# A two-layer encoder trunk: who updates x and applies norm weights at the layer boundaries

## Chip, cores and metric

One core of a Trainium2 chip. The metric is the device time of one execution, in microseconds; the comparison is between two programs that compute the same output. Engines: TensorE (PE, with its weight loads PEld), VectorE (DVE), ScalarE (ACT), GpSimd (POOL) and the queues that issue transfers (SyncE's is SP).

## The reference, cut to what matters

256 tokens with 2048 features pass two layers. Each layer has two sublayers: a mixer (GLA and neighbourhood attention in layer 0, a state-space mixer and sliding-window attention in layer 1) with one input and one output projection, and a dense SwiGLU feed-forward part (FFN). Each sublayer is normed on both sides:

```
for layer in range(2):
    h = rms_norm(x, g[0]);  mix = concat(mixers(h @ w_in)) @ w_out
    x = x + rms_norm(mix, g[1])
    h = rms_norm(x, g[2]);  f = (silu(h @ w_gate) * (h @ w_up)) @ w_down
    x = x + rms_norm(f, g[3])

def rms_norm(x, g):
    return x * rsqrt(mean(x * x, axis=-1) + 1e-6) * g
```

So there are four places where a projection's output is normed and added to x, and after the first three of them the new x is at once the input of the next norm. These three are the layer boundaries below.

## The kernel before

**Number format and tiles.** All products are float32 in accuracy: every operand is split into `hi` (rounded to the reduced float32 format, fp32r) and `lo` (the rest), and three matmuls stand for one: hi·hi, hi·lo, lo·hi. The tokens are two halves of 128 (t=0 and t=1); an x tile of one half has four pieces of 512 features (j = 0 to 3).

**Weights.** They are streamed from memory in chunks of 512 x 512, in order of use, in halves of 128x1024. `prep()` takes the next half in: `halves` casts it on ACT (`whi`, L199) and subtracts on VectorE (`wlo`, L201). `whi` and `wlo` have seven buffers each, so a cast may wait until TensorE has used an older half. `unit_a` runs the matmuls of one 512-column output: for each chunk the ones of t=0 (`part(0, ...)`, L227 to L229, 12 per chunk) are issued at once; the ones of t=1 are kept in a list (`pending`), up to four half chunks (6 matmuls each) behind.

**The end of a sublayer** (`post`). The output comes in four quarters (n = 0 to 3) per half. When a quarter of the last pass is done, `evac` adds it to `f` on VectorE (L444), sums its squares on ACT (L361) and multiplies it in place by the norm's weights `gb` (L492, on POOL for most quarters). With the fourth, `rstd` gets the scale `rs[t]`: a reduction and a mean on VectorE (L352, L356) and a power on POOL (L357). Then each piece of x is updated: x = x + rs·f (L465 ff.).

**The next norm** (`begin_norm`, `piece`). A generator of three steps per piece: four transposes on TensorE into one of four PSUM tiles (`tp`, L343); a product with the weights of the next norm on VectorE (`gx`, L385) and a cast to `hi` on ACT (`xt`, L387); a subtraction to `lo` on VectorE (`xt`, L390), with the sum of squares on ACT. The row scale of the next norm is applied behind its projection. At the start of the program the same generator runs for the input x, without an update of x (`START`).

**Order.** At a boundary the order is written by hand in `PROG`: X/x is the update of a piece, T/t its transposes, G/g the product and cast, L/l the subtraction, in capitals for t=0; `p` is one `prep()`, `q` the next half chunk that is pending. The first string runs at the end of the sublayer, the third after two chunks of the next stage. Which engine updates x is written in `XMODE` (d: one VectorE instruction; p: product and sum on POOL; a: product on ACT, sum on POOL; the third string is for t=1 of the very last sublayer). `pin` holds marked TensorE and VectorE instructions in program order during a boundary; the rest, all of ACT and POOL among it, is put in order by a planner of the framework, which follows priorities and its own estimates of time.

**Transfers.** Each updated piece of x is written to memory from the POOL queue (`xm`, `xf`) and read back by the end of the next sublayer; in the last sublayer it is the output, written from SP's queue.

Of the kernel before, what the change touches and what calls it, by code (L numbers as in the profile page):

```python
# [18 lines left out]
F32 = mybir.dt.float32  # L19
# [3 lines left out]
ALU = mybir.AluOpType  # L23
# [3 lines left out]
P = 128  # L27
# [23 lines left out]
LAG = 2  # L51
PSTT, PADD, PY, AY = (1, 2), True, True, 1
SY = 2
XMODE, MULP = ("ddpd", "daaa", "dadd"), True
PROG = ("X0 X1 p p X2 q X3 T0 q G0 T1 q G1 q T2 L0 p L1 x1 T3 x2 x3 G2 p p L2 G3 x0 p L3",
        "", "t0 t1 g0 l0 g1 t2 l1 g2 t3 l2 g3 l3")
START = ("T0 T1 G0 G1 L0 p L1", "t0", "g0 t1 l0 g1 l1", "p", "T2 T3 G2 G3 L2 t2 L3 t3", "g2 l2 g3 l3")
CONST_PARTS = {
# [36 lines left out]
class Trunk:  # L95
# [267 lines left out]
    def begin_norm(self, li, gi):  # L363

        nc = self.nc
        xt = ([None] * 4, [None] * 4, [None] * 4)
        rs = [None, None]
        ssp = [None, None]
        gain = self.gT[:, li * 2 + gi // 2]

        def piece(t, j, src):
            if xt[0][j] is None:
                xt[2][j] = self.s8.tile([P, 2, 4, T], F32R, tag="s8", name=self.nm("xt"))
                xt[0][j], xt[1][j] = xt[2][j][:, 0], xt[2][j][:, 1]
            if j == 0:
                ssp[t] = self.small([P, 4], "nss", "nss")
                rs[t] = self.keep.tile([P, 1], F32, tag="nrs", bufs=4, name=self.nm("nrs"))
            sl = slice(t * P, (t + 1) * P)
            hi, lo = xt[0][j][:, :, sl], xt[1][j][:, :, sl]
            with self.tc.high_priority(offset=NORM):  # L380
                ps = self.transpose4(src)
            yield
            with self.tc.high_priority(offset=NORM):
                gx = self.tmp([P, 4, P], nm="gx")
                self.pin(nc.vector.tensor_tensor(out=gx, in0=ps, in1=gain[:, 4 * j:4 * j + 4].unsqueeze(2)  # L385
                                                 .broadcast_to([P, 4, P]), op=ALU.mult))
                self.pin(nc.scalar.copy(hi, gx))  # L387
            yield
            with self.tc.high_priority(offset=NORM):
                self.pin(nc.vector.tensor_sub(lo, gx, hi.bitcast(F32)))  # L390
            self.sumsq(src, ssp[t][:, j:j + 1])
            if j == 3:
                self.rstd(ssp[t], 4, D, rs[t])
        return xt, rs, piece
# [13 lines left out]
    def post(self, li, gi, nseg, after, f=None, before=None):  # L408


        nc = self.nc
        given = f is not None
        f = f or [[None, None], [None, None]]
        gb = [None] * 4
        ssp = [self.small([P, 4], "pss", "pss") for _ in range(2)]
        rs = [self.small([P, 1], "prs", "prs") for _ in range(2)]
        state = {"si": 0}

        def reload():
            self.x = [[None, None], [None, None]]  # L420
            for t in range(2):
                for j in range(2):
                    self.load_x(t, j, nc.gpsimd)

        def seg(mk, xk):
            si = state["si"]
            state["si"] += 1
            last = si == nseg - 1
            if last:
                if before is None:  # L430
                    reload()
                for n in range(4):
                    gb[n] = self.mtmp([P, 512], nm="gb")
                    self.tc.keep_in_program_order(nc.gpsimd.dma_start(  # L434
                        out=gb[n], in_=self.dr["norm_gains"][li, gi, n * 512:(n + 1) * 512].partition_broadcast(P)))

            def add(t, ps, n, pin=False):
                if f[t][n // 2] is None:
                    f[t][n // 2] = self.slot([P, 1024], nm="f")
                d = f[t][n // 2][:, (n % 2) * 512:(n % 2) * 512 + 512]  # L440
                if si == 0 and not given:
                    nc.scalar.copy(d, ps)
                else:
                    i = nc.vector.tensor_add(d, d, ps)  # L444
                    if pin:
                        self.pin(i)
                return d

            live = {}

            def run(prog):

                for c in prog.split():
                    if c == "p":
                        self.prep()
                        continue
                    if c == "q":
                        self.pending.popleft()()
                        continue
                    t, j = int(c[0].islower()), int(c[1])  # L460
                    if c[0] not in "Xx":
                        if live[t, j] is not None:
                            next(live[t, j], None)
                        continue
                    s2 = slice((j % 2) * 512, (j % 2) * 512 + 512)  # L465
                    xs, d = self.x[t][j // 2][:, s2], f[t][j // 2][:, s2]
                    with self.tc.high_priority(offset=NORM):
                        mode = XMODE[2 if li == 1 and gi == 3 and t else t][j]
                        if mode != "d":
                            if mode == "a":  # L470
                                nc.scalar.mul(d, d, rs[t])
                            else:
                                nc.gpsimd.tensor_scalar(out=d, in0=d, scalar1=rs[t], scalar2=None, op0=ALU.mult)
                            nc.gpsimd.tensor_add(out=xs, in0=xs, in1=d)
                        else:
                            self.pin(nc.vector.scalar_tensor_tensor(out=xs, in0=d, scalar=rs[t], in1=xs,
                                                                    op0=ALU.mult, op1=ALU.add))
                        live[t, j] = after(t, j, xs)

            for n in range(4):  # L480
                def evac(t, ps, n=n):
                    if not last:
                        return add(t, ps, n)
                    if n == 3 and t == 0:
                        self.prep()
                        self.pinning = ("PE", "DVE")
                    with self.tc.high_priority(offset=NORM):
                        d = add(t, ps, n, n == 3)
                        self.sumsq(d, ssp[t][:, n:n + 1])
                        if n == 3:  # L490
                            self.rstd(ssp[t], 4, D, rs[t])
                        i = (nc.gpsimd if n < 3 or (t and MULP and not (li == 1 and gi == 3)) else nc.vector).tensor_mul(out=d, in0=d, in1=gb[n])  # L492
                        if n == 3:
                            self.pin(i)
                    if n == 3 and t == 0:
                        self.pinning = ("PE",)
                        self.pending.popleft()()
                        self.pending.popleft()()
                        self.pinning = ("PE", "DVE")
                if before is not None:  # L500
                    before(n)
                    if n == 2:
                        reload()
                if last and n == 2:
                    self.pinned = {}
                    self.pinning = ("PE",)
                self.unit_a(mk(n), xk, evac, len(mk(n)) - 1 if n == 1 else None)
            if last:
                run(PROG[0])
                assert not self.pending  # L510

                def end():
                    run(PROG[2])
                    self.pinning = ()
                self.pending.extend((lambda: run(PROG[1]), lambda: None, end, lambda: None))
        return seg
# [977 lines left out]
```

## Time and profile before

| | |
|---|---|
| median of 3 runs | 2202.31 us (2201.97 to 2202.34) |
| the profiled execution | 2202.5 us, span 2200.6 us |
| busy: PE / PEld / DVE / ACT / POOL | 2163.8 / 1804.1 / 1741.3 / 1212.2 / 212.9 us |
| mean granted clock of TensorE | 0.996 |
| the boundaries | about 417 to 450, 1132 to 1166 and 1464 to 1497 us |
| the last x update | 2191.6 to 2194.7 us |

The span is the time between the first and the last instruction of the profiled execution. An engine's busy time counts its instructions alone; a busy TensorE may still be at the lower of its two clocks (1.0 is 2.4 GHz, 0.5 is 1.2 GHz). In a row of the timeline the numbers are start and duration in us; a bracket gives the idle time of the engine ahead of it and what ended it. Instructions of one engine can overlap by some 0.1 us, and rows with xN are N instructions of one kind that follow one another.

### The profile page before, as it was taken

How to read it: one execution, taken by the hardware profiler on the slowest of the kernel's cores; microseconds unless marked ns; L12 is line 12 of the kernel's file. 1: busy time of each engine (PE TensorE's matmuls, PEld its weight loads, DVE VectorE, ACT ScalarE, POOL GpSimd, SP SyncE). 2: the span in 40 equal slices, each digit the busy share in tenths (PEclk: the TensorE clock that was granted, in tenths of full speed). 3: DMA queues.
4: the chain of work that ended last, by engine and by line, in shares of the span. 5: the costliest groups of instructions: out<-in, count | busy, mean ns of one | idle time of the engine just before them, and what ended most of it. 6: DMA issues, size and time to landing. Idle time of an engine off the chain costs nothing.

```text
span 2200.6 us, 28141 instructions
## 1 busy us (share of the span) xinstructions
PE 2163.8 (98%) x10416; PEld 1804.1 (82%) x10416; DVE 1741.3 (79%) x2119; ACT 1212.2 (55%) x1533; POOL 212.9 (10%) x246
## 2 busy tenths in 40 slices
PE   8999999999999999999999999999999999999997
PEld 7888888778888888888878988778888888888886
DVE  7888655766878888888878987776687889888885
ACT  6545445555565555556456455655556555555653
POOL 0001110310000000000031262221000000000003
PEclk9999999999999999999999999999999999999999
DMA  8444565574565655467466444557466565646744
GB/s 294 144 134 162 189 200 187 184 267 149 204 238 182 207 175 202 172 219 243 150 215 230 152 153 143 179 186 269 148 204 239 176 209 166 215 172 217 242 153 143
DMA packets 117321, 424.48 MB, mean 193 GB/s; under 512 B 13392, under 2 KB 13520, under 8 KB 117184
## 3 DMA queue, kind: packets, MB, share of 16 engines
q1 hardware_dynamic: 110592, 400.61, 53.8%
q0 software_dynamic: 6448, 21.99, 3.0%
q8 instruction: 81, 1.33, 0.2%
q14 instruction: 56, 0.46, 0.1%
q10 hardware_dynamic: 144, 0.10, 0.0%
HBM read 414.25 MB, written 8.39 MB: 192 GB/s over the span
## 4 chain that ended last, share of the span: by engine, by line
PE 92%; DVE 4%; issue 2%; ACT 1%; POOL 1%; DMA 0%; DVEq 0%; SPq 0%; POOLq 0%; ACTq 0%
PE acc L229 21%; PE acc L227 21%; PE acc L228 21%; PE sq L703 5%; PE sq L702 5%; PE sq L704 5%; PE acc L260 4%; PE acc L263 2%; DVE wlo L201 2%; PE tp L343 1%; DVE xt L390 1%; PE gs L903 1%; PE accb L300 1%; PE accb L301 1%; PE accb L302 1%
## 5 line engine op out<-in xcount | busy, mean ns | idle before, releaser
L201 DVE TENSOR_TENSOR wlo<-raw,whi 128x1024 fp32r<-128x1024 f32 x608 | 755.7, 1249 | 291.1 <-ACT whi L199 283.1
L199 ACT CAST whi<-raw 128x1024 fp32r<-128x1024 f32 x608 | 638.4, 1053 | 608.2 <-PE acc L229 399.0
L229 PE MATMUL acc<-whi,xt 128*128 128x512 f32 x1760 | 689.2, 392 | 7.9 <-DVE xt L390 7.9
L228 PE MATMUL acc<-wlo,xt 128*128 128x512 f32 x1760 | 686.9, 391 | 0.0
L227 PE MATMUL acc<-whi,xt 128*128 128x512 f32 x1760 | 678.8, 392 | 4.2 <-ACT xt L387 3.2
L229 PEld LDWEIGHTS acc<-whi,xt 128*128 128x128 f32 x1760 | 331.4, 188 | 79.8 <-DVE xt L390 11.1
L227 PEld LDWEIGHTS acc<-whi,xt 128*128 128x128 f32 x1760 | 331.6, 188 | 73.8 <-ACT xt L387 5.3
L228 PEld LDWEIGHTS acc<-wlo,xt 128*128 128x128 f32 x1760 | 331.4, 188 | 69.3 <-DVE wlo L201 0.8
L199 ACT CAST whi<-sw 128x1024 fp32r<-128x1024 f32 x252 | 265.7, 1054 | 207.4 <-PE acc L229 136.5
L201 DVE TENSOR_TENSOR wlo<-sw,whi 128x1024 fp32r<-128x1024 f32 x252 | 305.5, 1221 | 55.4 <-ACT whi L199 52.3
L703 PE MATMUL sq<-wlo,so 128*128 128x512 f32 x504 | 196.1, 389 | 0.0
L704 PE MATMUL sq<-whi,so 128*128 128x512 f32 x504 | 196.1, 389 | 0.0
L702 PE MATMUL sq<-whi,so 128*128 128x512 f32 x504 | 195.8, 390 | 0.0
L651 DVE TENSOR_TENSOR sw<-sw,sw 128x1024 f32<-128x1024 f32 x144 | 174.6, 1220 | 14.7 <-DMA sw<-sstream 14.0
L260 PE MATMUL acc<-xt,whi 128*128 128x512 f32 x384 | 138.0, 404 | 0.0
L434 POOL DMA_DIRECT2D gb<-norm_gains x16 | 8.7, 546 | 1194.0 <-DVE so L618 1180.9
L704 PEld LDWEIGHTS sq<-whi,so 128*128 128x128 f32 x504 | 94.6, 188 | 19.6
L702 PEld LDWEIGHTS sq<-whi,so 128*128 128x128 f32 x504 | 94.6, 188 | 19.4
L703 PEld LDWEIGHTS sq<-wlo,so 128*128 128x128 f32 x504 | 94.6, 188 | 19.4
L263 PE MATMUL acc<-xt,wlo 128*128 128x256 f32 x384 | 105.8, 286 | 0.0
L227 PE MATMUL acc<-whi,mixh 128*128 128x512 f32 x256 | 98.5, 396 | 0.6 <-ACT sz L788 0.6
L229 PE MATMUL acc<-whi,mixl 128*128 128x512 f32 x256 | 97.9, 391 | 0.0
(276 smaller groups left out, 2361.6 us busy)
## 6 DMA issues: line engine op xcount, KB each, us to landing
raw<-wstream SPq DMA_DIRECT2D x612, 512.0 KB, 4.8
sw<-sstream SPq DMA_DIRECT2D x144, 512.0 KB, 6.4
gb<-norm_gains POOLq DMA_DIRECT2D x16, 256.0 KB, 4.4
xm<-x POOLq DMA_DIRECT2D x16, 256.0 KB, 3.3
x<-xm POOLq DMA_DIRECT2D x8, 512.0 KB, 5.9
x<-x SPq DMA_DIRECT2D x4, 512.0 KB, 8.4
x<-x POOLq DMA_DIRECT2D x4, 512.0 KB, 7.4
xf<-x POOLq DMA_DIRECT2D x8, 256.0 KB, 3.4
```

The lines of the kernel that those rows point to most:

```text
L199: self.pin(nc.scalar.copy(hi, src))
L201: self.pin(nc.vector.tensor_sub(lo, src, hi.bitcast(F32)))
L227: self.pin(nc.tensor.matmul(ps[t], xh, wh[:, k % 2], start=s, stop=False))
L228: self.pin(nc.tensor.matmul(ps[t], xh, wl[:, k % 2], start=False, stop=False))
L229: self.pin(nc.tensor.matmul(ps[t], xl, wh[:, k % 2], start=False, stop=e))
L260: wide = lambda s, e: nc.tensor.matmul(ps, wh[:, kt % 8], self.joined(kt, xt), start=s, stop=e)
L263: nc.tensor.matmul(ps[:, 0], wl[:, kt % 8], xt[0][kt // 4][:, kt % 4, :], start=False, stop=False)
L300: nc.tensor.matmul(ps, wh[:, kt % 8], xh, start=kt == 0, stop=False)
L651: nc.vector.tensor_add(a, a, b)
L702: nc.tensor.matmul(ps, xh, wh[:, k], start=s, stop=False)
L703: nc.tensor.matmul(ps, xh, wl[:, k], start=False, stop=False)
L704: nc.tensor.matmul(ps, xl, wh[:, k], start=False, stop=e)
```

## The change

All updates of x are one VectorE instruction each (`XMODE` is gone). The products with `gb` of the quarters n=2 and 3 are on VectorE for both halves, n=0 and 1 stay on POOL (`MULP` is gone). In `piece` the weights of the next norm are no longer applied by a separate product: ACT makes `hi` from the transposed PSUM tile with the weight as its per-partition scale, and VectorE makes `lo` as tile x weight - hi, each in four instructions of 128 columns, since every 128 features have their own column of weights. The first string of `PROG` has a new order; the other strings stay.

```diff
-XMODE, MULP = ("ddpd", "daaa", "dadd"), True
-PROG = ("X0 X1 p p X2 q X3 T0 q G0 T1 q G1 q T2 L0 p L1 x1 T3 x2 x3 G2 p p L2 G3 x0 p L3",
+PROG = ("X0 X1 p X2 p p X3 T0 q G0 T1 q q G1 L0 T2 p L1 p T3 G2 q x0 L2 x1 p G3 x2 x3 L3",
         "", "t0 t1 g0 l0 g1 t2 l1 g2 t3 l2 g3 l3")
...
             yield
+            g = [gain[:, 4 * j + k:4 * j + k + 1] for k in range(4)]
             with self.tc.high_priority(offset=NORM):
-                gx = self.tmp([P, 4, P], nm="gx")
-                self.pin(nc.vector.tensor_tensor(out=gx, in0=ps, in1=gain[:, 4 * j:4 * j + 4].unsqueeze(2)
-                                                 .broadcast_to([P, 4, P]), op=ALU.mult))
-                self.pin(nc.scalar.copy(hi, gx))
+                for k in range(4):
+                    self.pin(nc.scalar.mul(hi[:, k], ps[:, k], g[k]))
             yield
             with self.tc.high_priority(offset=NORM):
-                self.pin(nc.vector.tensor_sub(lo, gx, hi.bitcast(F32)))
+                for k in range(4):
+                    self.pin(nc.vector.scalar_tensor_tensor(out=lo[:, k], in0=ps[:, k], scalar=g[k], in1=hi[:, k].bitcast(F32),
+                                                            op0=ALU.mult, op1=ALU.subtract))
...
                     with self.tc.high_priority(offset=NORM):
-                        mode = XMODE[2 if li == 1 and gi == 3 and t else t][j]
-                        if mode != "d":
-                            if mode == "a":
-                                nc.scalar.mul(d, d, rs[t])
-                            else:
-                                nc.gpsimd.tensor_scalar(out=d, in0=d, scalar1=rs[t], scalar2=None, op0=ALU.mult)
-                            nc.gpsimd.tensor_add(out=xs, in0=xs, in1=d)
-                        else:
-                            self.pin(nc.vector.scalar_tensor_tensor(out=xs, in0=d, scalar=rs[t], in1=xs,
-                                                                    op0=ALU.mult, op1=ALU.add))
+                        self.pin(nc.vector.scalar_tensor_tensor(out=xs, in0=d, scalar=rs[t], in1=xs,
+                                                                op0=ALU.mult, op1=ALU.add))
...
-                        i = (nc.gpsimd if n < 3 or (t and MULP and not (li == 1 and gi == 3)) else nc.vector).tensor_mul(out=d, in0=d, in1=gb[n])
+                        i = (nc.gpsimd if n < 2 else nc.vector).tensor_mul(out=d, in0=d, in1=gb[n])
```

## Rows read from the trace of the kernel before

**Rows 1.** The page: TensorE's busy time, and the chain of work that ended last by engine.

```profile
PE 2163.8 (98%) x10416; PEld 1804.1 (82%) x10416; DVE 1741.3 (79%) x2119; ACT 1212.2 (55%) x1533; POOL 212.9 (10%) x246
...
PE 92%; DVE 4%; issue 2%; ACT 1%; POOL 1%; DMA 0%; DVEq 0%; SPq 0%; POOLq 0%; ACTq 0%
```

**Rows 2.** Stretches of the three boundaries and one inside the second. Columns: stretch and its length, busy time and instructions of PE, PEld, DVE, ACT and POOL, TensorE's granted clock, the DMA share, GB/s.

```profile
410.00:450.00 40.00, 35.07 (x158) 26.54 (x157) 34.73 (x42) 24.93 (x49) 23.69 (x22) 1.00 0.55 187
1130.00:1168.00 38.00, 33.03 (x148) 25.74 (x147) 30.82 (x39) 23.14 (x47) 23.36 (x27) 0.96 0.65 227
1464.00:1500.00 36.00, 32.52 (x147) 25.50 (x147) 32.37 (x41) 23.43 (x43) 17.88 (x19) 0.95 0.55 187
...
1150.00:1152.50 2.50, 2.50 (x7) 1.93 (x7) 2.50 (x3) 0.73 (x3) 0.92 (x1) 0.50 0.53 167
```

**Rows 3.** TensorE in order of time at the boundaries: waits, and the last of the 25 matmuls that begin at 433.70.

```profile
424.06 0.66 PE L343 MATMUL tp<-ca,x 128*128 128x128 f32 x4 [0.51 <-DVE x L476]
...
433.70 0.50 PE L229 MATMUL acc<-whi,xt 128*128 128x512 f32 x1 [1.93 <-DVE xt L390]
...
439.16 0.39 PE L228 MATMUL acc<-wlo,xt 128*128 128x512 f32 x1
...
448.11 0.50 PE L229 MATMUL acc<-whi,xt 128*128 128x512 f32 x1 [0.69 <-DVE xt L390]
...
1148.70 0.50 PE L229 MATMUL acc<-whi,xt 128*128 128x512 f32 x1 [1.93 <-DVE xt L390]
...
1163.06 0.50 PE L229 MATMUL acc<-whi,xt 128*128 128x512 f32 x1 [0.98 <-DVE xt L390]
...
1494.13 0.50 PE L229 MATMUL acc<-whi,xt 128*128 128x512 f32 x1 [0.70 <-DVE xt L390]
```

**Rows 4.** VectorE at the boundaries in order of time (L444 the adds of output quarters, L476 updates of x, L201 `wlo`, L390 `lo`); the line that begins with L390 is all of it with the shortest, median and longest duration in ns, and the one behind it a stretch of the first boundary with the busy time of L390 alone.

```profile
419.67 0.68 DVE L444 TENSOR_TENSOR f<-f,acc 128x512 f32<-128x512 f32 x1
421.19 0.16 DVE L352 TENSOR_REDUCE ss<-pss 128x1 f32<-128x4 f32 x1 [0.85 <-ACT sq L361]
...
422.84 1.83 DVE L476 SCALAR_TENSOR_TENSOR x<-f,prs,x 128x512 f32<-128x512 f32 x2
424.59 3.44 DVE L201 TENSOR_TENSOR wlo<-raw,whi 128x1024 fp32r<-128x1024 f32 x2
427.96 1.78 DVE L476 SCALAR_TENSOR_TENSOR x<-f,prs,x 128x512 f32<-128x512 f32 x1
...
437.01 2.34 DVE L201 TENSOR_TENSOR wlo<-raw,whi 128x1024 fp32r<-128x1024 f32 x2
...
441.38 0.75 DVE L476 SCALAR_TENSOR_TENSOR x<-f,prs,x 128x512 f32<-128x512 f32 x1 [0.44 <-POOL prs L357]
...
446.23 1.82 DVE L390 TENSOR_TENSOR xt<-gx,xt 128x512 fp32r<-128x512 f32 x1 [0.69 <-ACT xt L387]
...
L390 DVE TENSOR_TENSOR xt<-gx,xt x32: 675/686/1837, 9.1 to 1502.7; 128x512 fp32r<-128x512 f32 x32
...
431.00:448.20 17.20, 7.63 (x5) 1.00 0.53 184
...
1134.36 0.69 DVE L444 TENSOR_TENSOR f<-f,acc 128x512 f32<-128x512 f32 x1 [2.03 <-PE acc L229]
...
1466.52 0.69 DVE L444 TENSOR_TENSOR f<-f,acc 128x512 f32<-128x512 f32 x1 [0.41 <-PE acc L229]
...
1471.45 4.61 DVE L201 TENSOR_TENSOR wlo<-raw,whi 128x1024 fp32r<-128x1024 f32 x1
```

**Rows 5.** POOL at the first and the third boundary in order of time (L492 products with `gb`, L474 sums of x).

```profile
424.96 1.99 POOL L492 TENSOR_TENSOR f<-f,gb 128x512 f32<-128x512 f32 x1
...
444.97 2.53 POOL L474 TENSOR_TENSOR x<-x,f 128x512 f32<-128x512 f32 x2
...
1471.82 1.30 POOL L492 TENSOR_TENSOR f<-f,gb 128x512 f32<-128x512 f32 x1
...
1473.65 1.31 POOL L474 TENSOR_TENSOR x<-x,f 128x512 f32<-128x512 f32 x1
```

**Rows 6.** Prices: `gx` over the whole run (shortest, median, longest in ns); the GLA output, four instructions in order of time; ACT instructions grouped by shape (busy us, mean ns of one, idle before); three scalings on ACT in order of time.

```profile
L385 DVE TENSOR_TENSOR gx<-tp,ca x32: 676/680/692, 6.7 to 1499.8; 128x512 f32<-128x512 f32 x32
...
162.99 1.13 DVE L994 SCALAR_TENSOR_TENSOR og<-go,grs,sg 128x128 f32<-128x128 f32 x4
...
L387 ACT CAST xt<-gx 128x512 fp32r<-128x512 f32 x32 | 19.6, 618 | 21.5 <-DVE gx L385 21.4
...
L788 ACT ACTIVATE nv<-acc,nrs 128x512 f32<-128x512 f32 x4 | 2.7, 684 | 2.9 <-PE acc L229 2.9
...
L1111 ACT ACTIVATE rq<-acc,nrs 128x256 f32<-128x256 f32 x2 | 0.9, 468 | 0.0
...
L471 ACT ACTIVATE f<-f,prs 128x512 f32<-128x512 f32 x10 | 6.6, 714 | 1.8 <-POOL prs L357 1.5
...
441.38 1.95 ACT L471 ACTIVATE f<-f,prs 128x512 f32<-128x512 f32 x3
```

**Rows 7.** The tail in order of time: the last updates of x on VectorE, and POOL's last sum.

```profile
2191.60 3.08 DVE L476 SCALAR_TENSOR_TENSOR x<-f,prs,x 128x512 f32<-128x512 f32 x3 [0.68 <-POOL prs L357]
...
2192.40 1.74 POOL L474 TENSOR_TENSOR x<-x,f 128x512 f32<-128x512 f32 x1 [0.83 <-ACT f L471]
```

**Rows 8.** The start: one stretch with the columns of rows 2, and the cast of a weight half behind it.

```profile
10.00:25.00 15.00, 15.00 (x74) 12.75 (x74) 14.62 (x23) 14.72 (x26) 3.94 (x6) 1.00 0.98 370
...
28.40 1.05 ACT L199 CAST whi<-raw 128x1024 fp32r<-128x1024 f32 x1 [3.26 <-DMA raw<-wstream]
```

## The prediction, made blind

> **What bounds the kernel now.** I read the busy shares and the chain first: TensorE is busy 98% of the span, and 92% of the chain that ended last lies on it [rows 1], so only stretches where it stands still can give time back. The table by stretch finds them at the layer boundaries: of 40, 38 and 36 us TensorE is idle 4.9, 5.0 and 3.5 us, while VectorE is busy 81 to 90%. In the second, TensorE also runs 2.5 us at a granted clock of 0.50 (the 1.2 GHz level) [rows 2], right behind a wait for VectorE of 1.93 us [rows 3]. So each boundary is a VectorE problem.
>
> TensorE's instructions in order of time show at which product it waits [rows 3]: 0.51 us for the first x update, 1.93 for the first `lo` of the next norm, and last 0.69, 0.98 and 0.70 us for the first `lo` of the second token half (t=1). From that last wait on it runs without a gap. I use that point, counted from the start of VectorE's add that ends the output quarter n=3 of t=0 (419.67, 1134.36, 1466.52 [rows 4]), as the measure of a boundary: 28.44, 28.70 and 27.61 us.
>
> VectorE's instructions say why it is late [rows 4]. The same x update takes 0.75 and 1.78 us; of 32 subtractions that make `lo` the median is 0.69 and the slowest 1.84; two `wlo` take 2.34 in one place, one alone takes 4.61 in another. Set beside POOL's [rows 5], every slow one shown overlaps a POOL product or sum and ends about its own length after POOL's end: the `lo` from 446.23 should end at 446.92; POOL's sums end at 447.50, `lo` at 448.05. The `wlo` from 1471.45 lies over two POOL instructions, the last of which ends at 1474.96, and it ends at 1476.06. VectorE instructions that read PSUM, as `gx` does, are never slow: 676 to 692 ns over all 32 [rows 6]. The Trainium skill ("SBUF — State Buffer", Who interferes with whom) has a rule for it: a VectorE instruction with two SBUF inputs and a GpSimd instruction that reads SBUF shut each other out, one with a single SBUF input doesn't take part. By that rule the new `lo` (one input in PSUM) can't be slowed and the new x updates can; the trace agrees, with the numbers just given.
>
> **The change, part by part.** Occupancies are start to start: `wlo` 1.13 us (two in 2.34, less the overlap of 0.08 that a following instruction has), an add or product 0.60, an x update 0.67 (0.75 less the same) [rows 4].
>
> *Late products and x updates.* POOL loses per boundary three products (n=2 of both t, n=3 of t=1), the pair that made X2 and three sums for x1 to x3; ACT loses three scalings, 1.95 us [rows 6]. VectorE gains 3 x 0.60 + 4 x 0.67 = 4.5 us. What it stops losing in the first boundary [rows 4]: X0 and X1 1.83 - 1.42 = 0.4, two `wlo` 3.44 - 2.34 = 1.1, X3 1.0, and five `lo` 7.63 - 5 x 0.69 = 4.2: 6.7 us. One POOL product stays inside the boundary (n=1 of t=1, 1.3 us as the one at 1471.82 [rows 5]); I charge one full hit of 1.3. At the other end it costs nothing, if `wlo` doesn't overlap it; in the first and third boundary a `wlo` did, so I take the hit.
>
> *Weights applied while splitting.* Per piece `gx` (0.60 of VectorE) goes, and one `lo` of 512 columns becomes four of 128 with a pointer scalar. The nearest row is the same form of instruction in the GLA output: four take 1.13 us [rows 6], 1.05 start to start. VectorE pays 1.05 for 1.20, a tie, but the four never wait for POOL, and the path VectorE, ACT, VectorE becomes ACT, VectorE. ACT pays more. With a pointer scale 256 columns from PSUM take 468 ns and 512 take 684, so 128 would take 360 (estimate on that line); three of 714 ns end in 1.95 us, so each hides 0.1 [rows 6], and four take 0.36 + 3 x 0.26 = 1.15 us against 0.62: for eight pieces 4.3 us more. From below it is nothing more than now. At the boundaries ACT is busy only 61 to 65% [rows 2], which covers it. The Trainium skill ("VectorE: DVE Perf Modes", The TRN2 errata) speaks against this part: every instruction pays a fixed latency, so tiles should not be cut below 512 elements. On ACT the rows agree (360 estimated for a quarter of what takes 684); on VectorE the saved `gx` pays for it.
>
> *Order.* Three `p` (a cast on ACT and a `wlo`) now stand among X0 to X3 instead of two; the first `q` (6 matmuls, 1.37 us) moves behind T0 and the last behind T3, so TensorE waits longer for X0 and has more to do later. The PSUM tile of a transpose is now held until its `lo` is done; there are four, and the fifth transpose waits for L0 only, long done.
>
> *The boundary in sum*, in us after the measuring point. X0 starts at 3.3 as now (422.84 - 419.67 = 3.2): the power on POOL is untouched, and the added product of t=0 fits into the 0.85 us in which VectorE waits for the sum of squares [rows 4]. If it gets ahead of the add, everything is 0.6 later. X0, X1 to 4.65; `wlo` with the hit 7.1; X2 7.75; two `wlo` 10.0; X3 10.7; add and product n=2 11.9; L0 12.95; `wlo` 14.1; L1 15.15; `wlo` 16.3; add n=3 16.9. Here a new wait stands: the statistics and the product n=3 wait for ACT's sum of squares (419.67 + 0.60 to 421.19: 0.9, I take 1), reduction, product and mean take 0.7, the power 0.7 (VectorE waits 0.68 for it in the tail [rows 7]); x0 starts at 19.35, and L2, x1, a `wlo`, x2, x3 and L3 queue behind it. x0 20.0, L2 21.05, x1 21.75, `wlo` 22.9, x3 24.2, L3 25.25, first `lo` of t=1 26.3. L0 is done about 1 us sooner than now (TensorE's wait for it ends at 433.70 [rows 3], 14.0 on this count), L3 no sooner; the gain is behind L3, where the `lo` of t=1 now ends at 28.4 (448.05).
> TensorE, with 24 matmuls in 5.46 us (0.2275 each [rows 3]) and 0.5 for a set of transposes: after 12 popped matmuls free at 2.5; T0 waits for X0 until 4.1 (1.6 us for 0.5 now); T0, q, T1, q, q, T2 to 9.75; T3 waits for X3 to 11.0, with the last q 12.9; 24 matmuls of the next stage to 18.35 (L0 and L1 are there); two more, wait for L2's first quarter to 20.35, the other ten to 22.65; two sets of transposes 23.6, two matmuls 24.05, wait for L3's first quarter to 24.55, six matmuls and a third set: 26.4. That state of work is the one of 28.44, 28.70 and 27.61: gains of 2.0, 2.3 and 1.2, together 5.5 us. Without the hit all from the first `wlo` on is 1.3 sooner: 9.4.
>
> *The tail.* Now the last x update waits until POOL's sum ends at 2194.14 and runs to 2194.68 [rows 7]. After: everything as now to 2191.60, then four updates to 2191.60 + 4 x 0.67 + 0.08 = 2194.36. The product n=2 falls into a wait of VectorE for ACT. Gain 0.3; 0.3 lost if it gets ahead of the add.
>
> *The start.* Eight pieces, no x updates. Between 10 and 25 us TensorE has no gap and ACT is busy 14.7 of 15 us [rows 8], so some of the added 4.3 us may show. But ACT waits 3.26 us behind that stretch for weights, and it has sums of squares in it that nothing needs soon. I take 0.5; ends 0 and 4.3.
>
> Sum: -5.5 - 0.3 + 0.5 = -5.3. The profiled execution took 2202.5 us (span 2200.6); the median of the runs is 2202.31, 0.2 below it. 2202.5 - 5.3 = 2197.2, so **2197.0 us** as a median.
>
> **The rivals.**
> *No hit at all* (20%). For: POOL's product must first wait for its sum of squares and for an issue of a transfer, and `wlo` may start ahead. Against: the two rows named. -9.4 - 0.3 + 0.5: 2193.1.
> *The start takes the gain* (22%). ACT's small instructions queue in order in front of the casts that TensorE needs; with 98% busy all 4.3 us can show: 2202.3 - 5.8 + 4.3 = 2200.8. The errata rule above makes this the likely one. For: that share; against: ACT's 3.26 us of idle time. The same result comes if the sum of squares of n=3 waits its turn on ACT and x0 with it, by 1.2 us at each boundary.
> *Half clock after the longer wait for T0* (inside the forecast's 50%). The clock fell behind the second boundary's 1.93 us, yet not behind the first's [rows 2, 3]. 2.5 us at half pace cost 1.25, most of which the later waits for L2 and L3 (1.5 + 0.5) swallow.
> *Slower* (8%). VectorE's slow instructions are not POOL's doing. Then the 6.7 us stay where 1.3 are charged, the 4.5 us come on top as reckoned, and each boundary ends 5.4 us later than in the sum: 3 x 5.4 - 5.3 = +10.9, 2213. It decides once more than about 3.1 us of the 6.7 stay (1.3 charged, 1.8 gained). Against: the pairs in [rows 4, 5].
>
> **How the numbers follow.** The forecast case has 50% and an own range of 2194.5 to 2199.5. Two thirds of it, and the first rival, lie more than 0.2% below 2202.3 (4.4 us, about what a measurement of this kernel can tell from no change): faster 0.33 + 0.20 = 0.53. Same 0.17 + 0.22 = 0.39, slower 0.08. The range of 2191.5 to 2203 leaves out the slower case and the ends of the others.
>
> **What would show it.** Right: at the boundaries one slow `wlo` or x update at most; `lo` in quarters of about 0.34 us, none slow; the 1.93 us wait for the first `lo` gone, a wait of about 1.6 for X0, waits for L2 or L3 still there; the measuring points about 2 us nearer. Wrong: slow VectorE instructions without POOL beside them, TensorE behind ACT in the first 30 us, the product n=3 waiting much over 1 us, or half clock in a stretch without gaps.

## The result, and the profile after

The changed kernel takes 2187.02 us (median of six, 2186.18 to 2191.97), the one before 2202.39 (2201.97 to 2203.28): a ratio of 0.9933 (95% 0.992 to 0.9946). Faster, as forecast, but by 15.4 us where 5.3 were forecast, and outside the range. The profiled execution took 2186.18, its span is 2184.4: 16.2 less than before's.

The page of the kernel after, TensorE and the others (compare [rows 1]):

```profile
PE 2154.6 (99%) x10416; PEld 1801.2 (82%) x10416; DVE 1732.4 (79%) x2208; ACT 1219.6 (56%) x1619; POOL 170.7 (8%) x217
```

The same 10416 matmuls keep TensorE busy 9.2 us less, and idle 7.0 us less. To see where, I cut both spans at E, the add that ends n=3 of t=0. VectorE of after in order of time, then the fourth E of before (the other three are in [rows 4]):

```profile
418.26 0.69 DVE L444 TENSOR_TENSOR f<-f,acc 128x512 f32<-128x512 f32 x1
...
1129.92 0.69 DVE L444 TENSOR_TENSOR f<-f,acc 128x512 f32<-128x512 f32 x1 [0.49 <-PE acc L228]
...
1455.17 0.69 DVE L444 TENSOR_TENSOR f<-f,acc 128x512 f32<-128x512 f32 x1 [0.41 <-PE acc L228]
...
2165.04 0.69 DVE L444 TENSOR_TENSOR f<-f,acc 128x512 f32<-128x512 f32 x1 [0.49 <-PE acc L228]
```

```profile
2180.40 0.69 DVE L444 TENSOR_TENSOR f<-f,acc 128x512 f32<-128x512 f32 x1 [2.03 <-PE acc L229]
```

| stretch | before | after | gain | forecast |
|---|---|---|---|---|
| start to E1 | 419.67 | 418.26 | 1.41 | -0.5 |
| E1 to E2 (first boundary) | 714.69 | 711.66 | 3.03 | 2.0 |
| E2 to E3 (second boundary, mixer of layer 1) | 332.16 | 325.25 | 6.91 | 2.3 |
| E3 to E4 (third boundary) | 713.88 | 709.87 | 4.01 | 1.2 |
| E4 to the end | 20.2 | 19.4 | 0.8 | 0.3 |

The boundaries by stretch in after, laid out from E as in [rows 2] (columns as there):

```profile
408.60:448.60 40.00, 36.51 (x176) 29.66 (x175) 36.18 (x72) 30.39 (x74) 11.07 (x15) 1.00 0.62 194
1125.60:1163.60 38.00, 34.49 (x166) 28.00 (x166) 31.45 (x69) 29.69 (x73) 12.42 (x20) 1.00 0.72 237
1452.60:1488.60 36.00, 33.98 (x165) 27.60 (x164) 32.67 (x67) 28.11 (x67) 6.66 (x12) 1.00 0.64 202
```

TensorE is idle 3.5, 3.5 and 2.0 us, 1.45 less in each, and its clock is 1.00 throughout. All waits of TensorE over 0.2 us at the three boundaries, in order of time (L342 are transposes):

```profile
422.39 0.66 PE L342 MATMUL tp<-ca,x 128*128 128x128 f32 x4 [1.45 <-DVE x L468]
429.31 0.66 PE L342 MATMUL tp<-ca,x 128*128 128x128 f32 x4 [1.25 <-DVE x L468]
438.03 0.66 PE L342 MATMUL tp<-ca,x 128*128 128x128 f32 x4 [0.79 <-DVE x L468]
...
1134.09 0.63 PE L342 MATMUL tp<-ca,x 128*128 128x128 f32 x4 [1.49 <-issue]
1140.95 0.66 PE L342 MATMUL tp<-ca,x 128*128 128x128 f32 x4 [1.22 <-DVE x L468]
1149.68 0.66 PE L342 MATMUL tp<-ca,x 128*128 128x128 f32 x4 [0.80 <-DVE x L468]
...
1459.35 0.63 PE L342 MATMUL tp<-ca,x 128*128 128x128 f32 x4 [1.49 <-issue]
1465.38 0.63 PE L342 MATMUL tp<-ca,x 128*128 128x128 f32 x4 [0.39 <-DVE x L468]
```

They are for T0, T3 and t0 (at the third boundary for T0 and T3). No wait for a `lo` is left; before, the first boundary had six waits, three of them shown in [rows 3]. The work by which the prediction measures a boundary (44 matmuls of the next stage and three sets of t=1's transposes) is behind TensorE when it starts the fourth set:

```profile
443.56 0.60 PE L342 MATMUL tp<-ca,x 128*128 128x128 f32 x4
```

This point is 25.30 us after E1, for 28.44 before. VectorE of the first boundary (L468 updates, L200 `wlo`, L389 `lo`, L351 the reduction for the mean square), with POOL's one product there:

```profile
421.59 1.41 DVE L468 SCALAR_TENSOR_TENSOR x<-f,prs,x 128x512 f32<-128x512 f32 x2
422.91 2.75 DVE L200 TENSOR_TENSOR wlo<-raw,whi 128x1024 fp32r<-128x1024 f32 x1
...
428.52 0.74 DVE L468 SCALAR_TENSOR_TENSOR x<-f,prs,x 128x512 f32<-128x512 f32 x1
429.18 1.11 DVE L389 SCALAR_TENSOR_TENSOR xt<-tp,ca,xt 128x128 fp32r<-128x128 f32 x4
...
437.23 0.75 DVE L468 SCALAR_TENSOR_TENSOR x<-f,prs,x 128x512 f32<-128x512 f32 x1
437.90 1.12 DVE L389 SCALAR_TENSOR_TENSOR xt<-tp,ca,xt 128x128 fp32r<-128x128 f32 x4
...
443.15 2.15 DVE L389 SCALAR_TENSOR_TENSOR xt<-tp,ca,xt 128x128 fp32r<-128x128 f32 x8
```

```profile
423.26 1.30 POOL L484 TENSOR_TENSOR f<-f,gb 128x512 f32<-128x512 f32 x1
```

One `wlo` is slow, and it lies over POOL's product; updates and `lo` are at full speed.

Two places of before where the clock was at half, by stretch (columns as above):

```profile
57.50:60.00 2.50, 2.50 (x9) 2.12 (x9) 0.62 (x2) 2.49 (x3) 0.00 (x0) 0.50 0.00 2
1480.00:1482.50 2.50, 2.20 (x5) 1.81 (x6) 2.50 (x4) 2.44 (x6) 0.75 (x1) 0.56 0.80 284
```

The first of these stretches in after:

```profile
57.50:60.00 2.50, 2.50 (x17) 2.21 (x16) 0.58 (x2) 2.48 (x3) 0.00 (x0) 1.00 0.07 28
```

With the one at 1150 [rows 2], before had three such places between start and tail, and after has none in its profiled execution. The clock of before is at 0.50 from 56.9 to 60.3, from 1149.2 to 1152.6 and from 1480.3 to 1483.7 us: at half pace up to 1.7 us lost at each.

VectorE in the tail of after, ahead of the last transfers:

```profile
2173.58 0.69 DVE L484 TENSOR_TENSOR f<-f,gb 128x512 f32<-128x512 f32 x1 [0.85 <-ACT sq L360]
2174.19 0.68 DVE L444 TENSOR_TENSOR f<-f,acc 128x512 f32<-128x512 f32 x1
...
2177.20 2.74 DVE L468 SCALAR_TENSOR_TENSOR x<-f,prs,x 128x512 f32<-128x512 f32 x4 [0.66 <-POOL prs L356]
```

### The profile page after: what moved, and what is told of

It reads as the page before. It is cut to its first block, busy times and chain, and to the rows that moved or that the text cites. A ratio compares the mean times of both kernels' runs of the same rounds, so it can differ in the third digit from the quotient of the medians.

```text
span 2184.4 us, 28289 instructions
## 1 busy us (share of the span) xinstructions
PE 2154.6 (99%) x10416; PEld 1801.2 (82%) x10416; DVE 1732.4 (79%) x2208; ACT 1219.6 (56%) x1619; POOL 170.7 (8%) x217
## 5 line engine op out<-in xcount | busy, mean ns | idle before, releaser
L200 DVE TENSOR_TENSOR wlo<-raw,whi 128x1024 fp32r<-128x1024 f32 x608 | 750.1, 1239 | 291.9 <-ACT whi L198 283.2
L200 DVE TENSOR_TENSOR wlo<-sw,whi 128x1024 fp32r<-128x1024 f32 x252 | 305.2, 1219 | 55.6 <-ACT whi L198 52.4
L695 PEld LDWEIGHTS sq<-wlo,so 128*128 128x128 f32 x504 | 94.6, 188 | 19.4
L694 PEld LDWEIGHTS sq<-whi,so 128*128 128x128 f32 x504 | 94.6, 188 | 19.4
```

Source lines behind the costliest of these rows:

```text
L200: self.pin(nc.vector.tensor_sub(lo, src, hi.bitcast(F32)))
L694: nc.tensor.matmul(ps, xh, wh[:, k], start=s, stop=False)
L695: nc.tensor.matmul(ps, xh, wl[:, k], start=False, stop=False)
```

## Experiments

**The three parts, one by one and two by two.** U: x updates and late products on VectorE. S: the weights applied while splitting. O: the new order. Each kernel has the hunks of the change that are named, and the old code elsewhere. Medians in us:

| | old split | new split (S) |
|---|---|---|
| neither U nor O | 2202.3 | 2192.1 |
| U | 2208.7 | 2201.8 |
| O | 2209.5 | 2194.1 |
| U and O | 2194.4 | 2187.0 |

The kernel before, measured again beside them, took 2202.3. In the profiles the clock is at 0.50 between start and tail for 10.2 us (neither), 23.9 (U), 13.7 (O) and 0 (U and O), and with S for 3.4, 20.5, 3.4 and 0 us. So the differences of the table hold waits and clock together.

*U alone*, 2208.67, ratio 1.0028 (1.0017 to 1.0039):

```diff
-                        mode = XMODE[2 if li == 1 and gi == 3 and t else t][j]
...
+                        self.pin(nc.vector.scalar_tensor_tensor(out=xs, in0=d, scalar=rs[t], in1=xs,
...
-                        i = (nc.gpsimd if n < 3 or (t and MULP and not (li == 1 and gi == 3)) else nc.vector).tensor_mul(out=d, in0=d, in1=gb[n])
+                        i = (nc.gpsimd if n < 2 else nc.vector).tensor_mul(out=d, in0=d, in1=gb[n])
```

> The kernel before with all x updates and the late products (n=2 and n=3) on VectorE; the norm's weights are still applied by the separate product gx, and the order of pieces is the old one. Theory A (POOL's products and sums slow VectorE, and that is most of the gain): the slow lo, wlo and x updates at the boundaries go away, at most one wlo per boundary stays slow, and the time is 6 to 10 us below the kernel before, 2192 to 2196. Theory B (the gain is the shorter path from the transposed tile to hi and lo): 0 to 3 us below, 2199 to 2202. Theory C (the planner's rearrangement and TensorE's clock, not the parts, make the sum): no saying for this part, but the parts do not add up to the whole. The half clock that the kernel before shows at 57 to 60.4 us stays, since nothing of the start is changed; the ones at 1149.6 and 1480 go with the waits ahead of them.

Theories A and B missed (C says nothing of this part): it is slower. ACT, VectorE and TensorE at the first boundary:

```profile
432.38 1.04 ACT L198 CAST whi<-raw 128x1024 fp32r<-128x1024 f32 x1 [2.32 <-DMA raw<-wstream]
```

```profile
434.08 0.69 DVE L483 TENSOR_TENSOR f<-f,gb 128x512 f32<-128x512 f32 x1 [2.88 <-ACT sq L360]
```

```profile
436.63 0.79 PE L228 MATMUL acc<-whi,xt 128*128 128x512 f32 x1 [5.77 <-DVE xt L389]
```

A weight cast on ACT waits for its transfer, the sum of squares stands behind it, a product on VectorE waits for that sum, and `lo` of the first piece stands behind the product: TensorE waits 5.77 us. The half clock at 1150 and 1480, expected to go, lasts twice as long instead, 6.8 us, and comes at the first boundary too (435.1 to 441.9). Of the 7.0 us by which this profile is longer than before's, TensorE is idle for 4.7 and busy for 2.3.

*S alone*, 2192.09, ratio 0.995 (0.9935 to 0.9965):

```diff
-                self.pin(nc.scalar.copy(hi, gx))
+                    self.pin(nc.scalar.mul(hi[:, k], ps[:, k], g[k]))
...
-                self.pin(nc.vector.tensor_sub(lo, gx, hi.bitcast(F32)))
+                    self.pin(nc.vector.scalar_tensor_tensor(out=lo[:, k], in0=ps[:, k], scalar=g[k], in1=hi[:, k].bitcast(F32),
```

> The kernel before with the norm's weights applied by ScalarE and VectorE while they split (gx gone, hi and lo in four instructions of 128 columns); x updates, products and order as before. Theory A: lo reads one operand from PSUM and is no longer slowed, which was 4.2 of the 6.7 us of the first boundary, but the x updates and wlo still are: 2 to 5 us below the kernel before at the boundaries, and the start costs 0.4: 2197 to 2200. Theory B: nearly the whole gain, 2187 to 2190. If the half clock at 57 to 60.4 us hangs on when the start's stretch comes, it is gone here and 1.6 us more are gained; if not, it is still there.

Better than theory A allowed: 10 us. In the first boundary TensorE's wait for `lo` falls from 1.93 to 0.33 us; E1 to E2 takes 3.9 less, E2 to E3 5.2, but E3 to E4 nothing. The third boundary says why; VectorE, then POOL, then ACT:

```profile
1461.15 5.74 DVE L201 TENSOR_TENSOR wlo<-raw,whi 128x1024 fp32r<-128x1024 f32 x2
```

```profile
1461.52 1.30 POOL L493 TENSOR_TENSOR f<-f,gb 128x512 f32<-128x512 f32 x1
...
1463.35 1.31 POOL L475 TENSOR_TENSOR x<-x,f 128x512 f32<-128x512 f32 x1
```

```profile
1470.12 1.05 ACT L199 CAST whi<-raw 128x1024 fp32r<-128x1024 f32 x1 [4.37 <-DMA raw<-wstream]
```

Two `wlo` lose 3.4 us to POOL, and a cast waits 4.37 us for weights. `lo` is never slowed, though 51 of its quarters lie beside a product or sum of POOL: these take 331 to 352 ns, the other 77 take 331 to 353 (shortest, median and longest of its 128 quarters in ns):

```profile
L390 DVE SCALAR_TENSOR_TENSOR xt<-tp,ca,xt x128: 331/342/353, 9.3 to 1490.1; 128x128 fp32r<-128x128 f32 x128
```

*O alone*, 2209.46, ratio 1.003 (1.0018 to 1.0041):

```diff
-PROG = ("X0 X1 p p X2 q X3 T0 q G0 T1 q G1 q T2 L0 p L1 x1 T3 x2 x3 G2 p p L2 G3 x0 p L3",
+PROG = ("X0 X1 p X2 p p X3 T0 q G0 T1 q q G1 L0 T2 p L1 p T3 G2 q x0 L2 x1 p G3 x2 x3 L3",
```

> The kernel before with the new order of pieces alone. Theories A and B: the order only moves the place of the same waits, 2201 to 2204. Theory C: 3 us or more to either side, with no change of the slow VectorE instructions. The half clock at 57 to 60.4 us stays.

Theory C's size, to the bad side: TensorE waits for X0 and X3 as in the changed kernel, reaches t0's transposes sooner and waits there too (2.74, 2.73 and 1.58 us). Its waits add up to 4.6, 7.0 and 6.8 us in the three boundaries, for 4.9, 5.0 and 3.4 before. The half clock at 57 us, expected to stay, is gone; four others are there.

*S and O, without U*, 2194.12, ratio 0.9961 (0.9946 to 0.9975); the second and third of these diffs.

> The changed kernel with x updates and late products back on POOL and ScalarE as before (new split form and new order stay). Theory A: slow x updates and wlo are back beside POOL's sums, lo in quarters of 0.34 us is not slowed; 5 to 9 us of the gain are lost, 2192 to 2196. Theory B: at most 3 us are lost, 2187 to 2190. No half clock at 57 us if the start's timing decides on it.

As theory A says. Three `wlo` take 5.68 us beside POOL (3.5 by their usual distance), while twelve quarters of `lo` beside POOL's sums run at full speed:

```profile
424.14 5.68 DVE L201 TENSOR_TENSOR wlo<-raw,whi 128x1024 fp32r<-128x1024 f32 x3
...
442.29 3.35 DVE L390 SCALAR_TENSOR_TENSOR xt<-tp,ca,xt 128x128 fp32r<-128x128 f32 x12
```

*S and U, without O*, 2201.75, ratio 0.9996 (0.9987 to 1.0005); the first and second.

> The changed kernel with the old order of pieces (x updates and late products on VectorE, new split form). With the updates and products alone VectorE stood at a late product that waited for ScalarE's sum of squares, which stood behind a cast that waited for weights, and lo stood behind that product. Theory D (the new order is what lets the updates on VectorE pay, because it puts x0 to x3 and the products behind L0 and L1): the waits for lo come back and most of the gain is lost, 2196 to 2204. Theory E (the split form is what lets them pay, since lo needs no gx ahead of it on VectorE and can go before those products): within 3 us of the changed kernel, 2184 to 2190.

Theory D. ACT and VectorE at the first boundary, then TensorE:

```profile
426.13 1.16 ACT L385 ACTIVATE xt<-tp,ca 128x128 fp32r<-128x128 f32 x4
...
432.51 1.04 ACT L198 CAST whi<-raw 128x1024 fp32r<-128x1024 f32 x1 [2.29 <-DMA raw<-wstream]
```

```profile
435.23 0.16 DVE L351 TENSOR_REDUCE ss<-pss 128x1 f32<-128x4 f32 x1 [4.29 <-ACT sq L360]
```

```profile
436.31 0.80 PE L228 MATMUL acc<-whi,xt 128*128 128x512 f32 x1 [6.33 <-DVE xt L389]
```

`hi` is ready at 427.3, but in the old order the last pending half chunk, and with it VectorE's add, statistics and products of t=1, stands ahead of L0. VectorE waits 4.29 us for a sum of squares that only the updates of t=1 need, and L0 stands behind it.

*U and O, without S*, 2194.38, ratio 0.9965 (0.9951 to 0.9979); the first and third.

> The changed kernel with the old split (separate product gx, one cast, one subtraction of 512 columns); x updates and late products on VectorE, new order. Theory D: the order is enough, 2188 to 2195, and TensorE's waits for lo stay under 1 us each. Theory E: lo waits for gx, ScalarE and its place in VectorE's order again, TensorE waits for lo by 2 us or more at each boundary, and the time is near or above the kernel before, 2199 to 2210.

Theory D again. Up to X3 it runs as the changed kernel to 0.2 us; then three `gx` and two `lo` ahead of x0 where the changed kernel has two sets of quarters put x0 at 19.9 us after E for 19.0, and the wait for t0 is 1.57 for 0.79.

**The updates alone**, 2208.16, ratio 1.003 (1.002 to 1.0041): U without its products.

```diff
-                        mode = XMODE[2 if li == 1 and gi == 3 and t else t][j]
...
+                        self.pin(nc.vector.scalar_tensor_tensor(out=xs, in0=d, scalar=rs[t], in1=xs,
```

> The kernel before with the x updates alone on VectorE; the late products n=2 and n=3 stay on POOL, old split, old order. With updates and products together (2208.7) VectorE stood 2.3 to 4 us in each boundary at a late product or a reduction that waited for ScalarE's sum of squares, and lo of the first piece stood behind it, so that TensorE waited up to 5.8 us for lo. Theory F (the late products are what lo queues behind): those waits fall below 2 us and the time is 2196 to 2203. Theory G (the updates of t=1, which stand ahead of L2 and L3 in the old order and wait for the statistics of t=1, are what costs): the time stays above 2205.

Theory G by the time, though the waits for `lo` did fall to about 1 us. A wait for `hi` took their place:

```profile
436.90 2.08 DVE L468 SCALAR_TENSOR_TENSOR x<-f,prs,x 128x512 f32<-128x512 f32 x3 [1.46 <-POOL prs L357]
```

```profile
440.28 0.80 PE L227 MATMUL acc<-whi,xt 128*128 128x512 f32 x1 [2.48 <-ACT xt L387]
```

x1 to x3 stand ahead of `gx` of the third piece and wait for the statistics of t=1. So updates and products each bring t=1's late statistics into VectorE's queue, ahead of t=0's split.

**POOL's last product away**, 2184.40 (2183.46 to 2185.59), ratio 0.992 (0.9906 to 0.9933): faster than both.

```diff
-                        i = (nc.gpsimd if n < 2 else nc.vector).tensor_mul(out=d, in0=d, in1=gb[n])
+                        i = (nc.gpsimd if n < 2 - t else nc.vector).tensor_mul(out=d, in0=d, in1=gb[n])
```

> The changed kernel with the product n=1 of t=1 on VectorE too, so that no POOL product lies inside the boundary. If the slow wlo (2.75 and 2.73 us at the first two boundaries, 1.22 to 1.23 elsewhere) is POOL's doing, it falls to about 1.2, VectorE pays 0.6 for the product, and X2, X3 and all behind them come 0.7 to 0.9 sooner at the first two boundaries; the third has no hit to lose and pays 0.6 or hides it. TensorE's wait for X3 falls from 1.25 to about 0.5: 1 to 2 us faster than the changed kernel, 2185 to 2186. If the slow wlo is not POOL's doing, it stays at 2.7 and the kernel is 1 to 2 us slower, 2188 to 2189.

VectorE and TensorE at the first boundary, and VectorE in the tail:

```profile
423.76 1.22 DVE L200 TENSOR_TENSOR wlo<-raw,whi 128x1024 fp32r<-128x1024 f32 x1
...
2167.45 2.74 DVE L468 SCALAR_TENSOR_TENSOR x<-f,prs,x 128x512 f32<-128x512 f32 x4
```

```profile
429.24 0.66 PE L342 MATMUL tp<-ca,x 128*128 128x128 f32 x4 [0.33 <-DVE x L468]
```

The slow `wlo` falls from 2.75 to 1.22 and the wait for X3 from 1.25 to 0.33; the second boundary does the same (1.22 to 0.30), the third, which had no hit, nothing. In the tail the four updates of t=0 take 2.74 us for 3.77: there, too, a product lay beside them.

**One more update off POOL**, 2195.05, ratio 0.9965 (0.9953 to 0.9977): S, and X2 of t=0 on VectorE.

```diff
-XMODE, MULP = ("ddpd", "daaa", "dadd"), True
+XMODE, MULP = ("dddd", "daaa", "dadd"), True
```

> The kernel before with the new split form and, of the updates, only X2 of t=0 moved from POOL to VectorE; t=1's updates, the products and the order as before. In the run with the split form alone, POOL's scaling, sum and product beside X0 to X3 made two wlo take 3.46, 4.78 and 5.74 us for 2.34, and one x update 1.78 for 0.75; the third boundary gained nothing. If that contention is what keeps it from the changed kernel's time: the two wlo fall to at most 3.7 in each boundary, X3 takes 0.75, the third boundary gains 2 to 4 us, and the time is 2186 to 2190. If the x updates of t=1 on ScalarE and POOL are what holds it, nothing changes: 2190 to 2193.

A miss, 3.0 us slower than S alone. The two `wlo` of the third boundary fell to 3.89 and X3 to its full speed, but TensorE now waits 2.22 us for x0: a cast on ACT again waits 4.30 us for weights, the sums of squares of x stand behind it, and on VectorE the reduction of these sums, which waits 2.99 us, stands ahead of x0. Behind that wait the clock is at half for 6.8 us (S alone: 3.4). So the late weights, and the clock behind them, take what less of POOL could give there.

**A later start**, 2202.82, ratio 1.0002 (0.9993 to 1.0011): the first cast twice.

```diff
 self.pin(nc.scalar.copy(hi, gx))
+if li == 0 and gi == 0 and t == 0 and j == 0:
+    self.pin(nc.scalar.copy(hi, gx))
```

> The kernel before with the very first cast to hi done twice, so that the whole start runs about 0.53 us later and does nothing else. In ten profiles the clock fell to half in the 55 to 60 us stretch where the last pair of the small gz matmuls began at 55.38 to 55.87 us (four of four) and not where it began at 56.29 to 56.95 (none of six). If it is the time at which that stretch comes that decides: the pair begins at about 56.4, the clock stays at 1.00 there, and the added 0.53 us gains about 1.1: 2201 to 2201.5 for 2202.3. If it is chance, the clock falls as before and the time is 0.5 longer: 2202.8.

Half right. The pair of `gz` came at 56.75, 0.9 us later and not 0.5, and the clock stayed at 1.00 there. But it fell elsewhere, also at the first boundary, where before's did not:

```profile
57.50:60.00 2.50, 2.50 (x15) 2.20 (x16) 0.92 (x2) 2.47 (x3) 0.00 (x0) 1.00 0.19 74
...
432.50:435.00 2.50, 2.11 (x7) 1.72 (x8) 2.50 (x3) 1.96 (x6) 1.91 (x1) 0.77 0.03 13
...
1147.50:1150.00 2.50, 2.13 (x5) 1.75 (x6) 2.50 (x3) 2.44 (x7) 1.24 (x1) 0.50 0.14 54
1382.50:1385.00 2.50, 1.84 (x5) 1.41 (x6) 2.08 (x12) 1.28 (x5) 0.00 (x0) 0.55 0.00 0
```

**Weights prepared later**, 2185.42, ratio 0.9922 (0.9908 to 0.9935), with POOL's product away as above.

```diff
-"X0 X1 p X2 p p X3 T0 q G0 T1 q q G1 L0 T2 p L1 p T3 G2 q x0 L2 x1 p G3 x2 x3 L3"
+"X0 X1 p X2 p q X3 T0 G0 T1 q p q G1 L0 T2 L1 p T3 G2 q x0 p L2 x1 p G3 x2 x3 L3"
```

> The changed kernel with the product n=1 of t=1 on VectorE and one preparation of weights (1.13 us of VectorE) moved from ahead of X3 to behind it, another from ahead of x0 to behind it, and one pending half chunk moved from behind T0 to ahead of it. By VectorE's order X3 comes 1.13 us sooner and x0 too, L0 at the same time; TensorE's waits for X0 and X3 (1.45 and 0.33) shrink to about 0.4 and nothing: 1.2 to 1.6 us per boundary, 2180 to 2182. If weights then come late or TensorE only waits elsewhere (for x0 or for wlo), there is no gain: 2183 to 2187.

No gain. The waits for X0 and X3 are gone; TensorE waits for x0 (1.59 us, 1.32 and 0.66 at the other boundaries) and `hi` of the third piece (0.46) instead:

```profile
436.58 0.66 PE L342 MATMUL tp<-ca,x 128*128 128x128 f32 x4 [1.59 <-DVE x L468]
437.69 0.79 PE L226 MATMUL acc<-whi,xt 128*128 128x512 f32 x1 [0.46 <-ACT xt L385]
```

In this profile the clock is at half from 437.5 to 440.9, behind these two waits, which costs up to 1.7 us. The stretches of the second and third boundary are 0.15 and 0.4 us shorter than with POOL's product away alone, so moving the waits may be worth some tenths of a us a boundary, which the clock hides in the median.

## Why the prediction was right and wrong

**Right: VectorE's schedule and POOL's part in it.** The hand schedule holds within about 1 us: X0 3.3 after E (forecast 3.3), end of X3 11.0 (10.7), end of L2 20.8 (21.05), end of L3 24.9 (25.25). T0 waits 1.45 us (1.6) and T3 until 11.05 (11.0). The hit charged is the hit found at the first two boundaries, on a `wlo`: 1.5 us for 1.3. Taking its POOL product away removes it, so POOL is its cause and the slower rival falls. The Trainium skill ("SBUF — State Buffer", Who interferes with whom) lets an instruction with one SBUF input run beside GpSimd; that agrees with the 51 quarters of `lo` at 331 to 352 ns beside POOL.

**Wrong: the waits for L2 and L3**, in the boundary's sum. I put 1.5 + 0.5 us there, with TensorE idle until each. The planner put t0's transposes ahead of the first matmul that needs L2's `lo`, and those of t1 and t2 ahead of the first that needs L3's: TensorE waits 0.79 us, for x0, and then no more. `PROG` fixes their order among themselves, not their place among the next stage's matmuls; I took the place of the kernel before. That term is 1.2 us too large, and the point of the first two boundaries comes at 25.30 us after E for the 26.4 of the sum.

**Wrong: a hit at the third boundary.** It did not come (`wlo` 1.22), and it could not: there the product n=1 of t=1 runs ahead of E, in before too (1461.06). The product at 1471.82, on which I read the price and the overlap, is that of n=2, which the change takes off POOL. T3 is 0.8 us sooner, t0 finds x0 ready, and the point comes at 23.78 us. A smaller slip: the point of 28.70 in the second boundary holds 44 matmuls but only two sets of transposes, so the gain there should have been some 0.4 us larger. (The 24 matmuls of 5.46 us, 25 in [rows 3], are 24 starts and 23 distances; the usual distance is 0.227 all the same.)

**Wrong: the clock at no price**, in the start's term. The sum has no term for it; a fall was only a rival's loss. Of before's three places the one at 57 us tells: TensorE has no gap there, and no wait behind it takes the loss up. After's profile lacks it, some 1.7 us, which covers the 1.41 us that came up to E1 where 0.5 were to be lost. The other two lie inside the second and third boundary and so in their points already. There the prediction's argument holds that later waits swallow most of the loss: the first boundary, without a fall, reaches its point at 28.44, the second, with one, at 28.70 and one set of transposes short. That the clock stays up in after because its waits are shorter or fewer is argued, not shown: the first boundary's 1.93 us had no fall behind it. And it differs between executions of one kernel: the mean granted clock is 0.996 to 0.999 in the six of after, and the longest of them, 2191.97, is the one of 0.996.

**Wrong by omission: the mixer of layer 1.** The stretch from 147 to 252 us behind E2, before and after:

```profile
1281.40:1386.40 105.00, 100.52 (x505) 83.83 (x505) 87.74 (x182) 56.81 (x104) 42.49 (x42) 1.00 0.43 142
```

```profile
1276.90:1381.90 105.00, 102.50 (x515) 85.74 (x513) 85.37 (x180) 58.75 (x109) 49.17 (x44) 1.00 0.40 132
```

2.0 us less idle, where the change edits nothing: two waits for ACT (0.94 and 0.63 us) and two smaller ones (0.49 and 0.34) are gone. All four kernels that have S and O together show 2.5 us of idle time here, all others 3.5 to 4.5. Why the planner's order comes out better with them was not settled.

The 16.2 us are then, in the prediction's own terms: 1.4 up to E1 (forecast -0.5); 3.1, 3.8 and 3.8 at the boundaries (2.0, 2.3 and 1.2); 3.0 between the second boundary's point and E3 (nothing); 0.8 in the tail (0.3); and 0.1 elsewhere, with rounding. Of the 3.0 the mixer's idle time is 2.0. The rest is busy time and goes with the four fewer waits: by records a wait costs TensorE more than its idle time, since a matmul starts 0.89 us ahead of the transposes that wait 0.51 (423.17 and 424.06) where 0.227 is the usual distance, and the one behind a wait is followed after 0.34 (433.70, 434.04). That is 0.27 us a wait (an estimate from these two).

**Wrong: the tail's reason.** The last update ends 14.9 us behind E, for 14.3 before and a forecast of 14.0: POOL's product slows the updates of t=0 (3.77 us), and the product n=2 gets ahead of the add (2173.58 and 2174.19), which the prediction set as a chance. Without POOL's product it ends at 13.9. The 0.8 us come behind it, where only transfers are left: 4.5 us for 5.9. Why these end sooner was not tried.

**Wrong: the split as "a tie".** VectorE's instructions cost what I said (four quarters 1.11 us, `gx` and `lo` 1.20), and with U and O the split form still gains 7.4 us, alone 10.2. What I named, the path through two engines instead of three legs, I did not price: `gx` of later pieces stands ahead of x0 in VectorE's queue (0.9 us), and behind L3 each `lo` waits for its own `gx` and cast (up to 0.69 us), where the quarters follow one another. The rule of the Trainium skill that the prediction weighed ("VectorE: DVE Perf Modes", The TRN2 errata) is told of instructions whose source is SBUF; here `hi` is made from PSUM alone and `lo` from one operand in each. It doesn't bite on VectorE, by the 1.11 us; on ACT a quarter takes 390 ns for the estimated 360, and TensorE's waits in the first 30 us are the same (1.47 us, and 1.25 + 0.20), so the start rival falls.

**Wrong in kind: pricing the parts as a sum.** U is worth +6.3 us alone and -7.1 beside S and O; O +7.2 alone and -14.7 beside S and U. U puts instructions that need the late statistics of t=1 into VectorE's queue. O moves the last pending half chunk, and with it these statistics and products, behind L0 and L1, and x1 to x3 behind L2. I saw the queue behind x0 (the new order's) but never asked what the same edit does in the old order, which would have shown how much hangs on the order. Why a weight cast waits for its transfer in those kernels (2.3 to 4.4 us) was not tried, and how much of each figure is clock was not told apart.

**The rivals.** No hit at all: the kernel without POOL's product is that case, 2.6 us below the changed one, where three hits were to be worth 3.9. In its profile 1.2 and 0.8 us are gained in the first two boundary stretches and 1.3 in the tail, 0.3 lost in the third, and 0.9 lost up to E1, where its clock falls. Half clock behind T0's wait: not in the profiled execution of after.

## What to carry to other kernels

In an engine that works in order, an instruction moved to it brings its own latest input into the queue: write down what stands behind it, in the old order and in the new, before summing durations. In a stage bound by one engine's queue, taking contention out of that queue ahead of what is waited for won 0.8 to 1.2 us at two boundaries here, moving the waits about nothing that the median shows. A place of half clock in the profile before is time that a change may give back where no wait stands behind it, though not surely. And before a row is charged as a price, look which instruction it is: the product read at the third boundary was one that the change takes away.

## What the runs showed of the hardware

The clock can fall in a stretch in which TensorE never waits: in before it is at half from 56.9 to 60.3 us, and TensorE is busy without a gap from 30 to 62. At 53 to 56 us it runs small `gz` matmuls (16 rows) between large ones. In the profiles of thirteen kernels the clock fell behind the last pair where it began at 55.38 to 55.87 us (four of four), and not where it began at 56.29 to 56.95 (none of nine). The later start fits this, but doesn't show that the time alone decides. At its start matmuls stand 0.43 us apart, the half pace, until 14.0 us, in before until 12.4. In the four that fell this pace ends at 11.7 to 12.6 us, in eight of the others at 13.5 to 14.7. Only S alone tells the two apart (11.9, and no fall with the pair at 56.38), in one execution. Nothing was won by the later start, since the clock fell at other places.
